# 36 weight pieces of the second block split during the last feed-forward stage and kept in HBM, and one column multiplied once

## The chip, the cores and the metric

The kernel runs on one core of a Trainium2 chip. The metric is the device time of one execution in microseconds (us), as the median of several runs. The core has five engines, each with its own queue of instructions: TensorE (PE, matrix products), VectorE (DVE), ScalarE (ACT), GpSimd (POOL) and SyncE (SP, which here only starts DMAs). DMAs are started from SP, ACT or POOL.

## The reference

512 tokens of 1024 channels go through a first block of two layers and then through a second block. All numbers are float32.

```python
def first_block(x, mem, ...):
    for layer in range(DEPTH):                       # 2
        mix = mixer_ab(...) if layer % 2 == 0 else mixer_c(...)
        x = layer_norm(alpha * x + mix, ...)
        x = layer_norm(alpha * x + cross_attend(x, mem, ...), ...)
        x = layer_norm(alpha * x + conv_ffn(x, ffn_w_up[layer], ...), ...)
    return x

def conv_ffn(x, w_up, conv_w, conv_b, w_down):       # D_FF = 2816 = 22 x 128
    up = x @ w_up
    a, g = up[..., :D_FF], up[..., D_FF:]
    g = causal_dwconv(g, conv_w) + conv_b
    return (jax.nn.gelu(g) * a) @ w_down

def second_block(x, c, ...):                         # one layer
    shift, scale, gate = jnp.split(silu(c) @ w_ada[l] + b_ada[l], 3, axis=-1)
    h = rms_norm(x, norm_g[l]) * (1.0 + scale) + shift
    proj = h @ w_in[l]                               # r, k, v, g, decays; q, k, v, g of the attention
    ps = token_shift(proj[..., :D_SHIFT], mu_shift[l])
    y_r, g_r = rwkv7_mix(ps, ...)                    # a recurrence over the tokens, 8 heads of 64
    y_a = chunk_band_attention(q, ka, va, ...)       # 8 heads of 64
    y = concat([y_r * silu(g_r), y_a * silu(g_a)])
    return x + gate * (y @ w_out[l])
```

## The kernel before

**Products.** PE keeps the accuracy of float32 by splitting each operand into a rounded part `hi` and a rest `lo` and adding three products (`mm3`, lines 263 to 265: `hi*hi`, `hi*lo`, `lo*hi`). A weight matrix comes in *pieces* of 128 x 1024 numbers, 512 KB: one piece is one column block of 128 outputs over all 1024 inputs (for the values of the attention, 256 inputs by 512 outputs), and a piece makes 8 x 3 = 24 products of 128 x 512.

**From a piece to a weight.** `piece` (line 238) takes a buffer `raw` and a slot of the ring of weights (`wtile`), starts the load into `raw` on SP, and calls `split`: ACT copies `hi` into the slot (line 229), and the rest is subtracted by DVE in the first block and by POOL in the second (line 230). In the first block `raw` has three buffers (`raw` 2, `rawx` 1) and the ring six slots (`w` 4, `wx` 2); in the second, two and four.

**The order.** The Tile framework's planner puts the instructions of each engine into a fixed order before the run. It follows the order in which the program emits them as a priority, but takes what is ready by its own estimate of durations; a tile with a tag and `bufs=n` has n buffers, and an instruction waits until one is free. Waits at run time hold up everything behind them on the same engine.

**The last feed-forward** (`ffn(1, ...)`, 1050 to about 1400 us) goes in three chunks of 8, 8 and 6 hidden tiles of 128 channels (`CHUNKS`). An *up stretch* makes two column blocks for each hidden tile f (gate, then value), with ACT and DVE doing the convolution and the gelu behind them (lines 631 to 639) and a split of the result into a tile `hd`. A *down stretch* makes 8 column blocks over the chunk's hidden tiles and adds them to `x` on DVE (lines 645 to 652). The two big tiles `vt` (1 MiB each) hold attention values earlier on and lie idle during this stage.

**The start of the second block.** In `open2`, during the last norm, the column blocks 16, 0, 4, 8 and 1 (`OPEN`) are multiplied by halves of the tokens.

**The second block** (`block2`) has one line of work with long waits, which is emitted at a raised priority: for each of four pairs of heads `rwkv_pair` (a chain through ACT, DVE, POOL and PE, with PE's bonus product at `pb` waiting for DVE's line 894), then `rwkv_invert` (62 steps on DVE, lines 1003 and 1005, between two round trips through HBM), then `rwkv_chain`. All other work is *filler*: `ORDER` lists it by the milestone from which it may be emitted, `bg` holds it as generators, and `fill(us)` emits about that much of it at a place where the line waits. In `ORDER`, r, q, g are column blocks of w_in (each through `lin_g`), v the values (`att_v`, each weight piece read for two halves), p and a the attention, o the start of the output product (`out_begin`, four columns over their first six inputs, whose weights stay in all four slots of `w`), which `out_end` finishes before it makes columns 4 to 7. The entry r1 makes column block 1 again, though `open2` has made it.

Column blocks that `rwkv_epi` shifts go into the ring `rk` of six tiles.

Of the kernel before, what the change touches and what calls it, by code (L numbers as in the profile page):

```python
# [48 lines left out]
    (0, "r1"), (0, "r5"), (0, "r9"),  # L49
# [123 lines left out]
class Prog:  # L173
# [69 lines left out]

    def raw(self):
        self.n += 1
        if self.extra and self.n0 % 3 == 2:
            self.n0 += 1
            return self.t("rawx", [P, 1024], F32, 1)
        self.n0 += 1
        return self.keep.tile([P, 1024], F32, tag="raw", name=f"raw_{self.n}", bufs=2)  # L250

    def wtile(self):
        """The weights' ring: some of its room is there only in the first block."""
        self.nw += 1
        if self.extra and self.nw % (4 + self.extra) >= 4:
            return self.t("wx", [P, 2, 1024], F32R, self.extra)
        self.n += 1
        return self.keep.tile([P, 2, 1024], F32R, tag="w", name=f"w_{self.n}", bufs=4)
# [8 lines left out]
    def lin(self, src, ms, xs, epi, n=S, first=0, last=0):  # L267
        """The first (last) few blocks go through one half of the tokens, then through the other, for the LN
        before (after) them; epi(m, psum, tokens) gets the last ones by halves."""
# [43 lines left out]
    def flush(self):  # L313
        """The LN that is due."""
        while self.pending:
            ts = self.pending.pop(0)
            self.ln_half(ts)
            if self.norm[0] == "ln_ffn_g" and self.norm[2] == 1:
                self.modulate(ts)

    def lin_tm(self, src, pieces, xs, ntok, epi):
        """out[tok tiles][128, 512 cols]: activations stationary, weights moving."""
        banks = [self.bank() for _ in range(ntok)]
        for j, pc in enumerate(pieces):
            w = self.piece(self.a[src][pc])
            for kk in range(2):
                k = 2 * j + kk
                cs = slice(kk * 512, kk * 512 + 512)
                for s in range(ntok):
                    ss = slice(s * P, s * P + P)  # L330
                    self.mm3(banks[s], (xs[k][0][:, ss], xs[k][1][:, ss]), (w[:, 0, cs], w[:, 1, cs]),
                             k == 0, k == 7)
        for s in range(ntok):
            epi(s, banks[s])
# [8 lines left out]
    def rsqrt(self, y, t, v, eps):  # L343
        """y = (v + eps) ** -0.5: the table's value and a Newton step; eps is a column of self.eps."""
# [7 lines left out]
    # residual, then LN over the channels  # L352
# [61 lines left out]
    # mixer of layer 0  # L414
# [204 lines left out]
    def ffn(self, l, xs):  # L619
        nc = self.nc  # L620
        for c, (f0, f1) in enumerate(CHUNKS):
# [3 lines left out]
            def epi(m, ps, ts):  # L625
# [9 lines left out]
                else:  # L635
                    h = self.tmp()
                    nc.vector.tensor_tensor(out=h, in0=ps, in1=keep["g"], op=ALU.mult)
                    hs.append(self.split(self.hd(), h))

# [5 lines left out]
            def epi_d(m, ps, ts):  # L645
# [5 lines left out]
                if c == 1 and l == 0 and m == 1:  # L651
                    self.ada_end()
                if c == 2:
                    self.res_stat(m, ts)
# [5 lines left out]
    # the modulation of the second block, gathered a piece at a time  # L660
# [23 lines left out]
    def ada_end(self):  # L684
        nc = self.nc
        # the sum over the partitions: within 32 of them by turning 32-blocks, then over the four groups
# [18 lines left out]
    def modulate(self, ts):  # L705
        """rms_norm(x) * norm_g * (1 + scale) + shift of half of the tokens."""
# [16 lines left out]
    def open2(self):  # L723
        """The second block's first products, of the first half of the tokens."""
# [48 lines left out]
    # The second block has one line of work with long waits (the states) and much other work for the tensor  # L773
    # engine: `bg` holds the latter as generators, and fill() puts some of it wherever the former waits.
# [57 lines left out]
    def mm(self, out, **kw):  # L832
        """A product on the line with the waits: it stays behind what fill() put before it."""
        self.tc.keep_in_program_order(self.nc.tensor.matmul(out, **kw))  # L834
# [4 lines left out]
    def lin_g(self, src, m, xs, epi, ks=range(KT)):  # L839
        w = self.piece(self.a[src][m])  # L840
# [25 lines left out]
    def rwkv_pair(self, j):  # L866
        """What the chunks of heads 2j and 2j+1 need."""
# [9 lines left out]
        # kk  # L877
# [12 lines left out]
        # k'  # L890
        nc.scalar.activation(u, av, AF.Identity, bias=self.ka1[:, j : j + 1], scale=self.v("k_a_2", j))
        nc.vector.tensor_tensor(out=k, in0=k, in1=u, op=ALU.mult)
        # bonus
# [7 lines left out]
        # decays  # L901
# [20 lines left out]
        # values by token  # L922
# [20 lines left out]
        # scores within the chunks  # L943
# [25 lines left out]
        # keys by token  # L969
# [10 lines left out]
        # the part of the right sides that no state enters  # L980
# [10 lines left out]
    def rwkv_invert(self, prs):  # L991
        """(I - N)^-1 of each chunk's strictly triangular N: 32-blocks by substitution, then the block between."""
# [58 lines left out]
    def rwkv_chain(self, prs, tt):  # L1051
# [40 lines left out]
        def line(i, pr):  # L1092
            for _ in chunks(i, pr):
                yield FILL[9]
            # group norm, then the gate
# [33 lines left out]
    def att_v(self, half, xs):  # L1129
        """Values of two token tiles."""  # L1130
        self.va += [self.t("va", [P, S], F32, 4) for _ in range(2)]
        banks = [self.bank() for _ in range(2)]
        for jj in range(4):
            w = self.piece(self.a["in_va"][jj])
# [12 lines left out]
    def att_epi(self, m, ps):  # L1147
        """Queries or keys of a pair of heads, normed."""
# [15 lines left out]
    def att_probs(self, j):  # L1164
        """Softmax of a pair of heads: a tile holds a chunk's queries of one head, then of the other."""
# [60 lines left out]
    def gate_epi(self, n):  # L1226
        """silu(x) = (tanh(x / 2) + 1) * x / 2; the half comes where it is used."""
# [22 lines left out]
    def out_begin(self):  # L1250
        """The residual, and the first products of w_out over what is there."""
# [5 lines left out]
        for m in range(NPART):  # L1257
            w, ps = self.piece(self.a["out"][m]), self.bank(("mm", "mm", "ch", "ch")[m])
# [9 lines left out]
    def out_end(self, out):  # L1268
        nc = self.nc
        rest = [k for k in range(KT) if k not in KS]  # L1270
        for m in range(8):
# [4 lines left out]
            else:  # L1276
                w, ps = self.piece(self.a["out"][m]), self.bank()
# [93 lines left out]
```

## Time and profile before

| | us |
|---|---|
| median of 3 runs | 1856.47 (1854.88 to 1857.15) |
| span of the profiled execution, first to last instruction | 1854.5 |
| PE busy | 1786.7 |
| DVE busy | 1096.3 |
| ACT busy | 783.0 |
| POOL busy | 362.8 |

The median of the runs is 2.0 us above the span of the profiled execution. A profile's page gives shares over the whole span; the views behind it can be asked for a stretch. In them a group of instructions is named by engine, line, operation, out<-in by the program's names (buffer numbers left out), then shapes and count; then the busy time and the mean of one; then the idle time of the engine ahead of them and what ended it. PE's matrix products are pipelined, so that their shown durations overlap: the distance from start to start tells what one costs. PEld is the loading of weights into PE. The granted clock of PE is shown as a share of 2.4 GHz: 0.50 is 1.2 GHz. A wait for several things is put down to the one that came last.

### The profile page before, as it was taken

To read this page: it belongs to the slowest core of one execution; us is meant where nothing else is said; L and a number is where in the kernel's file an instruction comes from. 1 tells how busy PE (TensorE), PEld (TensorE's weight loads), DVE (VectorE), ACT (ScalarE), POOL (GpSimd) and SP (SyncE) were. 2 spreads that over 40 slices of the span, in tenths; PEclk is the share of its full clock that TensorE was granted. 3 is DMA by queue.
4 is the path that set the end of the run, shared out by engine and by line. 5 is a ranking of instruction groups with operands and counts; after the bars stand their busy time and mean duration, and the time that the engine had idled before them with its cause. 6 is when DMAs were issued, how large, how long until landed. Compare 5 with 4: busy or idle time off the path is not lost.

```text
span 1854.5 us, 26344 instructions
## 1 busy us (share of the span) xinstructions
PE 1786.7 (96%) x10476; PEld 1502.4 (81%) x10476; DVE 1096.3 (59%) x1741; ACT 783.0 (42%) x1319; POOL 362.8 (20%) x331
## 2 busy tenths in 40 slices
PE   8999998999999999999999999999998888879999
PEld 7889988888888888988998988888887766656657
DVE  5676689743463467444565764343447666975673
ACT  5444534532332356232453642232335645535561
POOL 0115014000000051000501400000015455623232
PEclk9999999999999999999999999999999999989999
DMA  8431455332322226333131242323222222222142
GB/s 279 145 103 60 132 181 188 100 102 91 102 92 91 80 64 196 112 96 100 59 104 35 69 125 92 102 92 100 88 86 73 82 75 88 89 74 81 56 160 103
DMA packets 62635, 192.25 MB, mean 104 GB/s; under 512 B 7344, under 2 KB 10032, under 8 KB 62512
## 3 DMA queue, kind: packets, MB, share of 16 engines
q1 hardware_dynamic: 54432, 172.25, 29.0%
q0 software_dynamic: 3248, 9.44, 1.5%
q10 hardware_dynamic: 4832, 8.88, 1.4%
q8 instruction: 82, 1.34, 0.3%
q14 instruction: 41, 0.34, 0.1%
HBM read 181.36 MB, written 9.18 MB: 103 GB/s over the span
## 4 chain that ended last, share of the span: by engine, by line
PE 76%; DVE 15%; ACT 3%; issue 3%; DMA 2%; POOL 0%; SPq 0%; DVEq 0%; ACTq 0%; POOLq 0%
PE ch L264 10%; PE ch L263 10%; PE ch L265 10%; PE mm L263 9%; PE mm L265 9%; PE mm L264 9%; PE pv L264 3%; PE pv L263 3%; PE pv L265 3%; PE ch L834 3%; DVE x L401 2%; DVE xh L405 1%; DVE w L230 1%; DVE x L400 1%; DVE vt L681 1%
## 5 line engine op out<-in xcount | busy, mean ns | idle before, releaser
L263 PE MATMUL mm<-xh,w 128*128 128x512 f32 (+1 forms) x704 | 266.1, 378 | 8.5 <-ACT w L229 7.5
L265 PE MATMUL mm<-xh,w 128*128 128x512 f32 (+1 forms) x704 | 258.6, 367 | 0.8 <-DVE w L230 0.8
L264 PE MATMUL mm<-xh,w 128*128 128x512 f32 (+1 forms) x704 | 259.0, 368 | 0.0
L370 POOL TENSOR_TENSOR t<-x,x 128x512 f32<-128x512 f32 x6 | 8.1, 1351 | 1011.1 <-ACT w L229 656.1
L229 ACT CAST w<-raw 128x1024 fp32r<-128x1024 f32 (+2 forms) x131 | 133.1, 1017 | 164.0 <-PE ch L265 62.9
L263 PEld LDWEIGHTS mm<-xh,w 128*128 128x128 f32 x704 | 135.6, 193 | 35.7 <-ACT w L229 7.8
L264 PE MATMUL ch<-xh,w 128*128 128x512 f32 (+1 forms) x432 | 154.1, 357 | 0.6 <-DVE xh L405 0.5
L264 PEld LDWEIGHTS mm<-xh,w 128*128 128x128 f32 x704 | 135.9, 193 | 22.9 <-issue 3.4
L263 PE MATMUL ch<-xh,w 128*128 128x512 f32 (+1 forms) x432 | 153.0, 354 | 1.3 <-ACT xh L404 1.3
L265 PE MATMUL ch<-xh,w 128*128 128x512 f32 (+1 forms) x432 | 152.7, 353 | 1.5 <-DVE w L230 1.5
L265 PEld LDWEIGHTS mm<-xh,w 128*128 128x128 f32 x704 | 135.8, 193 | 22.6 <-issue 1.1
L229 ACT CAST wx<-raw 128x1024 fp32r<-128x1024 f32 (+1 forms) x85 | 88.1, 1039 | 152.4 <-PE ch L265 71.5
L230 DVE TENSOR_TENSOR w<-rawx,w 128x1024 fp32r<-128x1024 f32 (+2 forms) x85 | 104.1, 1225 | 68.0 <-ACT w L229 67.6
L229 ACT CAST w<-rawx 128x1024 fp32r<-128x1024 f32 (+2 forms) x85 | 87.3, 1027 | 116.4 <-PE mm L265 71.0
L230 DVE TENSOR_TENSOR w<-raw,w 128x1024 fp32r<-128x1024 f32 (+2 forms) x90 | 113.0, 1257 | 37.8 <-ACT w L229 37.4
L230 DVE TENSOR_TENSOR wx<-raw,wx 128x1024 fp32r<-128x1024 f32 (+1 forms) x85 | 107.6, 1267 | 27.6 <-ACT wx L229 27.4
L230 POOL TENSOR_TENSOR w<-raw,w 128x1024 fp32r<-128x1024 f32 x41 | 100.4, 2456 | 119.0 <-ACT w L229 115.1
L263 PE MATMUL ch<-xh,wx 128*128 128x512 f32 (+1 forms) x304 | 103.5, 341 | 0.0
L265 PE MATMUL ch<-xh,wx 128*128 128x512 f32 (+1 forms) x304 | 103.0, 339 | 0.0
L264 PE MATMUL ch<-xh,wx 128*128 128x512 f32 (+1 forms) x304 | 103.0, 339 | 0.0
L263 PE MATMUL mm<-hd,w 128*128 128x256 f32 (+1 forms) x304 | 97.7, 322 | 3.6 <-ACT hd L229 3.6
L265 PE MATMUL mm<-hd,w 128*128 128x256 f32 (+1 forms) x304 | 97.9, 322 | 0.0
(484 smaller groups left out, 4498.6 us busy)
## 6 DMA issues: line engine op xcount, KB each, us to landing
raw<-in_up SPq DMA_DIRECT2D x56, 512.0 KB, 3.5
rawx<-in_up SPq DMA_DIRECT2D x32, 512.0 KB, 3.5
kt<-in_ada SPq DMA_DIRECT2D x48, 256.0 KB, 3.3
raw<-in_dn SPq DMA_DIRECT2D x24, 512.0 KB, 3.5
raw<-in_in_r SPq DMA_DIRECT2D x24, 512.0 KB, 3.5
raw<-in_c_in SPq DMA_DIRECT2D x16, 512.0 KB, 3.5
raw<-in_xo SPq DMA_DIRECT2D x12, 512.0 KB, 3.6
raw<-in_xv SPq DMA_DIRECT2D x11, 512.0 KB, 4.1
```

What stands on the lines that cost most here:

```text
L229: nc.scalar.copy(hi, src)
L230: (eng or nc.vector).tensor_tensor(out=lo, in0=src, in1=f32(hi), op=ALU.subtract)
L263: mm(out, lhsT=ah, rhs=bh, start=start, stop=False)
L264: mm(out, lhsT=ah, rhs=bl, start=False, stop=False)
L265: mm(out, lhsT=al, rhs=bh, start=False, stop=stop)
L370: eng.tensor_tensor(out=sz, in0=self.x[0][:, ts] if m == 1 else sz, in1=z, op=ALU.add)
L400: (nc.vector if k in DVE_SUB else nc.gpsimd).tensor_tensor(out=x, in0=x, in1=mn, op=ALU.subtract)
L401: nc.vector.scalar_tensor_tensor(out=x, in0=x, scalar=gk, in1=rs, op0=ALU.mult, op1=ALU.mult)
L405: nc.vector.scalar_tensor_tensor(out=lo, in0=x, scalar=bk, in1=f32(hi), op0=ALU.add, op1=ALU.subtract)
L681: nc.vector.scalar_tensor_tensor(out=dst, in0=raw, scalar=sc, in1=dst, op0=ALU.mult, op1=ALU.add)
L834: self.tc.keep_in_program_order(self.nc.tensor.matmul(out, **kw))
```

## The change

The column block r1 is taken out of `ORDER`. During the last feed-forward, 36 of the second block's weight pieces are loaded, split and written back to HBM as pairs (`hi`, `lo`), one after another: `pre_begin` lists them in the order of their use, and `pre_step` is called once for each hidden tile of an up stretch and once for each column block of the first two down stretches, 38 times in all. A step starts the load of the next piece into the second half of a tile `vt` from POOL's queue and, for the piece of the step before, lets ACT copy `hi` into the first half, POOL subtract `lo` in place, and POOL's queue store both halves (1 MiB). In the second block `ready` loads a pair straight into a slot of `w` from SP's queue, in place of `piece`: 40 loads of 1 MiB, since the 4 pieces of the values are read twice. The remaining lines of the diff only shorten comments.

```diff
 ORDER = (
-    (0, "r1"), (0, "r5"), (0, "r9"),
+    (0, "r5"), (0, "r9"),
...
+    def pre_begin(self):
+        self.prep, todo = {}, []
+        for _, ws in ORDER:
+            for w in ws.split("+"):
+                k, m = w[0], int(w[1:])
+                if k in "rq" and m not in OPEN:
+                    todo.append(("in_r", m))
+                elif k == "g":
+                    todo.append(("in_r", 12 + m) if m < 4 else ("in_ga", m - 4))
+                elif w == "v0":
+                    todo += [("in_va", i) for i in range(4)]
+                elif k == "o":
+                    todo += [("out", i) for i in range(8)]
+        self.todo, self.due2 = todo, []
+
+    def pre_step(self):
+        nc = self.nc
+        if self.todo:
+            key = self.todo.pop(0)
+            t = self.t("vt", [P, 2, D], F32, 2)
+            nc.gpsimd.dma_start(out=t[:, 1, :], in_=self.a[key[0]][key[1]])
+            self.due2.append((key, t))
+        if len(self.due2) > 1 or not self.todo:
+            for key, t in self.due2[:1]:
+                self.due2.pop(0)
+                hi, lo = t[:, 0, :].bitcast(F32R), t[:, 1, :].bitcast(F32R)
+                nc.scalar.copy(hi, t[:, 1, :])
+                nc.gpsimd.tensor_tensor(out=lo, in0=t[:, 1, :], in1=t[:, 0, :], op=ALU.subtract)
+                name = f"sp_{key[0]}{key[1]}"
+                d = self.prep[key] = self.dram.tile([P, 2, D], F32, tag=name, name=name)
+                nc.gpsimd.dma_start(out=d, in_=t)
+
+    def ready(self, src, m):
+
+        w = self.wtile()
+        self.nc.sync.dma_start(out=f32(w), in_=self.prep[src, m])
+        return w
+
...
     def ffn(self, l, xs):
         nc = self.nc
+        if l == 1:
+            self.pre_begin()
...
                     hs.append(self.split(self.hd(), h))
+                    if l == 1:
+                        self.pre_step()
...
+                if c < 2 and l == 1:
+                    self.pre_step()
                 if c == 2:
                     self.res_stat(m, ts)
...
     def lin_g(self, src, m, xs, epi, ks=range(KT)):
-        w = self.piece(self.a[src][m])
+        w = self.ready(src, m)
...
-            w = self.piece(self.a["in_va"][jj])
+            w = self.ready("in_va", jj)
...
-            w, ps = self.piece(self.a["out"][m]), self.bank(("mm", "mm", "ch", "ch")[m])
+            w, ps = self.ready("out", m), self.bank(("mm", "mm", "ch", "ch")[m])
...
-                w, ps = self.piece(self.a["out"][m]), self.bank()
+                w, ps = self.ready("out", m), self.bank()
```

## Rows read from the trace of the kernel before

**Rows 1.** The page, part 1: busy us, share, count of each engine.

```profile
PE 1786.7 (96%) x10476; PEld 1502.4 (81%) x10476; DVE 1096.3 (59%) x1741; ACT 783.0 (42%) x1319; POOL 362.8 (20%) x331
```

**Rows 2.** Stretches: from:to, length, each engine's busy us, clock, DMA share, GB/s.

```profile
1094.00:1380.00 286.00, 286.00 (x1251) 234.64 (x1250) 121.89 (x141) 86.51 (x107) 0.00 (x0) 1.00 0.29 94
1440.00:1661.00 221.00, 190.51 (x1035) 144.47 (x1033) 164.95 (x262) 108.93 (x158) 112.67 (x79) 0.92 0.26 82
...
1780.00:1854.00 74.00, 67.58 (x305) 51.44 (x303) 39.29 (x53) 27.07 (x34) 20.37 (x11) 1.00 0.32 111
```

**Rows 3.** PE's waits from 1440 to 1700 us: total, times, longest.

```profile
PE ch L834 <- DVE rt L894: 17.8, 4, 4.9
PE at L1157 <- ACT t L1153: 6.0, 2, 5.8
```

**Rows 4.** The stretches at half clock from 1435 us on, as in rows 2.

```profile
1435.60:1442.40 6.80, 6.10 (x16) 5.03 (x17) 3.22 (x7) 4.27 (x11) 0.00 (x0) 0.50 0.40 135
...
1633.50:1640.30 6.80, 3.34 (x6) 2.01 (x7) 6.59 (x12) 3.22 (x5) 2.36 (x1) 0.50 0.00 0
1654.00:1660.80 6.80, 5.30 (x14) 3.98 (x14) 4.04 (x7) 0.63 (x1) 3.52 (x9) 0.50 0.44 125
sum 40.80, PE 33.53 PEld 22.94 DVE 32.56 ACT 10.81 POOL 21.35; mean PE 4.79 PEld 3.28 DVE 4.65 ACT 1.54 POOL 3.05
```

**Rows 5.** POOL's groups from 1100 us on, shapes apart.

```profile
L230 POOL TENSOR_TENSOR w<-raw,w 128x1024 fp32r<-128x1024 f32 x41 | 100.4, 2456 | 119.0 <-ACT w L229 115.1 <-DMA raw<-in_in_r 3.5
...
L966 POOL DMA_DIRECT2D dn<-mk x16 | 9.3, 588 | 12.2 <-DVE mk L960 12.2
```

**Rows 6.** DVE in time, about the inversion: start us, us, line, operation.

```profile
1604.40 4.37 DVE L349 TENSOR_SCALAR t<-t 128x512 f32<-128x512 f32 x1
...
1610.95 2.33 DVE L1003 TENSOR_TENSOR rt<-c,c 128x87 f32<-128x87 f32 x1
...
1615.67 0.28 DVE L1003 TENSOR_TENSOR rt<-c,c 128x112 f32<-128x112 f32 x1
...
1633.15 0.42 DVE L349 TENSOR_SCALAR t<-t 128x512 f32<-128x512 f32 x1
```

**Rows 7.** POOL in time, in the inversion.

```profile
1610.74 4.79 POOL L230 TENSOR_TENSOR w<-raw,w 128x1024 fp32r<-128x1024 f32 x2 [2.28 <-ACT w L229]
```

**Rows 8.** DVE in time, in pair 0.

```profile
1471.97 2.07 DVE L921 COPY pc<-rt 128x8 f32<-128x8 f32 x1
...
1476.23 2.96 DVE L894 SCALAR_TENSOR_TENSOR rt<-rk,vec,rk 128x512 f32<-128x512 f32 x1
```

**Rows 9.** POOL in time, in pair 0.

```profile
1471.15 2.85 POOL L230 TENSOR_TENSOR w<-raw,w 128x1024 fp32r<-128x1024 f32 x1
```

**Rows 10.** ACT in time, in pair 0.

```profile
1468.95 1.04 ACT L229 CAST w<-raw 128x1024 fp32r<-128x1024 f32 x1
```

**Rows 11.** PE in time, as output column 4 starts.

```profile
1828.86 0.39 PE L263 MATMUL mm<-ar,w 128*128 128x512 f32 x1
...
1831.58 0.39 PE L263 MATMUL mm<-xh,w 128*128 128x512 f32 x1
```

**Rows 12.** Filler ahead of pair 0's bonus product: PE, PEld, DVE, ACT on tiles mm.

```profile
1461.60:1479.30 17.70, 12.69 (x52) 9.69 (x52) 1.13 (x3) 1.38 (x2) 1.00 0.34 114
```

**Rows 13.** DVE's groups from 1440 us on, shapes apart.

```profile
L1113 DVE SCALAR_TENSOR_TENSOR yy<-yy,sav 128x512 f32<-128x512 f32 x4 | 4.8, 1195 | 0.1
```

**Rows 14.** DVE in time, where the first up stretch turns to down.

```profile
1135.86 0.68 DVE L230 TENSOR_TENSOR hd<-t,hd 128x512 fp32r<-128x512 f32 x1
```

**Rows 15.** PE in time at that turn: the last hidden tile's first product.

```profile
1138.33 0.39 PE L263 MATMUL pv<-hd,wx 128*128 128x512 f32 x1
```

**Rows 16.** ACT in time: the first slot's cast after the partial columns.

```profile
1825.03 1.06 ACT L229 CAST w<-raw 128x1024 fp32r<-128x1024 f32 x1 [6.65 <-PE mm L265]
```

**Rows 17.** DMA issues: out<-in, queue, count, KB each, median us to landing.

```profile
raw<-in_out SPq DMA_DIRECT2D x8, 512.0 KB, 3.6
...
dt<-c POOLq DMA_DIRECT2D x1, 512.0 KB, 2.9
```

## Prediction: what the change does to the time

> **What bounds the kernel now.** I read the page's busy shares first: TensorE (PE) is busy for 1786.7 us of a span of 1854.5 [rows 1], so a change pays only where it takes products away, closes an idle gap of PE or ends a stretch at the lower clock. The table of stretches says where those are [rows 2]. In the last feed-forward (1094 to 1380 us) PE is busy for 286.00 of 286 us, ScalarE (ACT) for 86.51, VectorE (DVE) for 121.89, GpSimd (POOL) for 0.00. In the second block up to the end of the inversion (1440 to 1661 us) PE is busy for 190.51 of 221 us at a granted clock of 0.92: 30.5 us are idle. The list of waits names the gaps [rows 3]: 17.8 us in four waits for the bonus input of a pair (DVE L894), 6.0 for the norm of a query or key (L1157). Behind such gaps the clock is down at 1.2 GHz: seven stretches of 40.8 us, the first in the norm before the block, with 33.53 us of busy PE [rows 4]. The six inside the block hold 33.53 - 6.10 = 27.4 us, which cost half of that, 13.7.
>
> **What stretches those chains.** Each of the 41 pieces of the block costs POOL a subtract of 2.456 us, 100.4 us in all [rows 5], and ACT a cast of 1.04. In the inversion a DVE step of 0.28 us or less takes 2.33 when a subtract runs beside it [rows 6, 7]: the step at 1610.95 us ends where the first of two subtracts ends. There are five such steps, each some 2.1 us too long, 10.6 in all, and just before them one norm step of L349 takes 4.37 us where it needs 0.42 at 1633.15: 3.9 more. In pair 0 the copy L921, of 8 columns, takes 2.07 us and ends with the subtract that runs from 1471.15 to 1474.00 us; L892, next on DVE, is late with it, and ACT's cast at 1468.95 us stands ahead of the exponential that L921 needs [rows 8 to 10].
>
> **The change part by part.**
> *r1 gone.* 24 products fall away; twelve take 1831.58 - 1828.86 = 2.72 us [rows 11], so **5.4 us**. No wait loses its cover, since filler isn't bound to its place: before pair 0's bonus product 52 filler products ran [rows 12], while the budgets of the two fills ahead of it (1.12 and 3, at 0.65 a step) make 2 + 5 steps, 21 products. The planner brought work forward, and can bring r2.
>
> *Pair waits.* Without subtract and cast L921 needs no more than 0.28 us and L892 starts some 1.9 earlier. What stays is POOL's own work of a pair, behind which L894 takes 2.96 us [rows 8]. So 4 x 1.9 = **7.6 us** of 17.8. Bounds: nothing, if POOL's pair products, freed, collide earlier; all 17.8, if L894 too finds POOL free.
>
> *Clock in the pairs.* The four low stretches behind them hold 33.53 - 6.10 - 3.34 - 5.30 = 18.8 us of busy PE [rows 4], 9.4 lost. The gaps that I leave are about 2.5 us each. Whether the clock falls behind those no row tells: the tail has 6.4 idle us at a clock of 1.00 [rows 2], in smaller gaps. I take half, **4.7 us**, with 0 and 9.4 as ends.
>
> *Inversion.* 14.5 us come off DVE, more than the 6.0 us for which PE waits for norms queued behind these steps. I take **5.9 us**, and 1.7 for half of the 3.34 at the low clock behind it: **7.6**.
>
> *Tail.* L1113 takes 1195 ns on average [rows 13] where a split of the same size with two inputs takes 0.68 us [rows 14]: 4 x 0.5, **2.0 us**.
>
> *Added to the feed-forward.* 36 x 1.04 = 37 us of ACT, 36 x 2.456 = 88 us of POOL, and 72 POOL DMAs at 0.59 us of issue [rows 5], 42 us. The cover is 200 idle us of ACT and an idle POOL. The DMA engines move 94 GB/s at a share of 0.29 [rows 2], 324 when full; 36 x 1.5 MiB over some 300 us add 189: 283. In a down stretch, with a step per 5.6 us, the demand is 375, which lags some 7 us behind by its end; the next up stretch takes that back. The weights are safe: six slots, five pieces ahead, 28 us. A stall can come where up turns to down: the last hidden tile is split until 1136.54 us and needed at 1138.33 [rows 14, 15], 1.8 us of slack. A cast and a subtract ahead of it (1.04 + 2.42) would stall 1.7. Between 0 and 3 x 1.7 I take **+1.5 us**. The Trainium skill, "SBUF — State Buffer", section "Who interferes with whom", makes the ports that VectorE and GpSimd share an exclusive lock, also against a VectorE instruction with two SBUF inputs. That rule speaks against the change, since the splits of the feed-forward are such instructions and meet no POOL today; the inversion's rows agree with it (2.33 us for 0.28). By it every turn would pay and the term be 5.1.
>
> *Loads of 1 MiB.* They go straight into a slot of `w`, of which there are four. In full work a piece lasts 5.4 us and three lie ahead, 16 us: covered. In `out_end` all four hold partial columns. The first is free when its cast starts, at 1825.03 us, and column 4 starts at 1828.86 [rows 11, 16]: 3.8 us. 512 KB land in 3.6 us [rows 17], so 1 MiB in 3.6 to 7.2; at 324 GB/s the second half adds 1.6. I take 5.2, so **+1.4 us** (0 to 3.4). The Trainium skill, "DMA: Bandwidth & Descriptors", section "Bandwidth", gives 6.15 us for 1 MB (from GpSimd's queue, not SP's): by it the term would be 2.4; no row shows it. The inversion's own DMAs now meet larger ones: **+1 us** (0 to 3).
>
> *Sum.* 5.4 + 7.6 + 4.7 + 7.6 + 2.0 = 27.3 gained, 3.9 lost: 23.4. The span becomes 1831.1; the median of the runs, 1856.47, lies 2.0 above today's span: **1833 us**.
>
> **The rivals.**
> *Gaps close wholly.* Idle 30.5, low clock 13.7, r1 5.4, tail 2.0, less 3.9: 47.7, **1809 us**. For it: a weight subtract stands ahead of the four waits. Against: L894's own delay behind POOL's pair products.
> *Gaps form again.* POOL's pair products start earlier and hold DVE as long, and the clock stays low: r1, half of the inversion and the tail are left, 5.4 + 3.8 + 2.0 - 3.9 = 7.3: **1849 us**. For it: L894 at 2.96 us with no weight subtract beside it. Against: L921, where one was.
> *The preparation stalls the feed-forward.* On POOL's one queue a step loads piece n, then subtracts and stores piece n-1; with two `vt` buffers load n waits for store n-2. If this order stays as written, a step lasts the subtract, two issues and the store: 2.5 + 1.2 + S. 512 KB are stored in 2.9 us [rows 17], so S is 2.9 to 5.8 and a step 6.6 to 9.5 us, against 5.6 in a down stretch and 11.2 in an up stretch. ACT's added casts then wait for POOL, with the casts of the weights queued behind them. After two down stretches with an up between, the lag is 24p - 179: 28 us, the weights' whole lead, at a step of p = 8.6. From there it costs: 21 us at 9.5, 38 at 10.2 with contention, and the clock with it. Price 40: **1873 us**. Against it: the planner brings forward what is ready, and with the subtract ahead of the waiting load two buffers, each round some 12 us, make 6 to 7 us a step.
>
> **How the numbers follow.** Forecast (1833, by itself 1822 to 1843) 0.55; gaps form again 0.20; gaps close 0.12; stall 0.10; the prepared pieces save nothing anywhere 0.03. The range holds the forecast, the re-formed gaps and what lies just short of full closing, 1811 to 1851, and leaves out the stall and the far end. A measurement of this kernel tells 0.2%, 3.7 us, from no change. Faster by more: 0.55 + 0.20 + 0.12 = 0.87; same 0.03; slower 0.10.
>
> **What would show it.** Right: no weight subtract on POOL in the block, inversion steps all under 0.5 us, pair waits of 2 to 3 us, PE full from 1094 to 1380 us with some 88 us of POOL beside it. Wrong: idle PE at an up-to-down turn, or in the second down stretch with ACT waiting for a DMA into `vt`; L894 still 3 us late; products that wait for a DMA into `w` anywhere but ahead of column 4.

## The result, and the profile of the changed kernel

The changed kernel takes 1888.1 us (median of 4 runs, 1880.9 to 1892.2) against 1855.7 for the kernel before: a ratio of 1.017, with an interval of 1.015 to 1.019. It is 32 us slower, where the forecast was 23 us faster. The time lies outside the range on record (1811 to 1851). Nearest to what happened is the rival called "the preparation stalls the feed-forward", which had a chance of 0.10 and a price of 1873 us. ScalarE is held up by the added casts, as it says; but what TensorE then waits for are hidden tiles, from the first down stretch on, where the rival had the weights run out late.

The profiled execution spans 1887.2 us, 32.7 more than before. Its busy shares answer to [rows 1]: TensorE does 24 products fewer, and is busy 2.5 us longer all the same.

```profile
span 1887.2 us, 26394 instructions
PE 1789.2 (95%) x10452; PEld 1501.9 (80%) x10452; DVE 1092.7 (58%) x1739; ACT 777.9 (41%) x1313; POOL 389.0 (21%) x398
```

The next table splits the span at points that both traces have: the first product of the cross-attention's output, the three down stretches (products on the tiles `hd`), and the first product of the second block's chain (the helper `mm`, L834 before, L879 after). All numbers are differences of starts and ends in the traces.

| stretch, us | before | after | difference |
|---|---|---|---|
| cross-attention's output to first down stretch | 142.1 | 157.6 | +15.5 |
| first down stretch | 45.0 | 71.7 | +26.7 |
| second up stretch | 86.9 | 98.5 | +11.6 |
| second down stretch | 44.9 | 52.2 | +7.3 |
| from there to the chain's first product | 150.4 | 146.4 | -4.0 |
| second block | 393.9 | 368.0 | -25.9 |

The block gained 25.9 us, and the stages ahead of it lost 57.1. The table of stretches says the same of TensorE (columns as in [rows 2]: from:to, length, each engine's busy us, granted clock, DMA share, GB/s). First the stretch that was full before, then the first down stretch alone, and below it the same down stretch in the kernel before:

```profile
1094.00:1380.00 286.00, 251.79 (x1059) 202.02 (x1059) 130.72 (x121) 99.28 (x117) 90.99 (x77) 0.92 0.64 228
1150.40:1222.10 71.70, 48.82 (x194) 37.76 (x193) 26.27 (x23) 20.76 (x23) 27.93 (x24) 0.81 0.66 244
```

```profile
1133.40:1178.40 45.00, 45.00 (x194) 36.20 (x194) 15.92 (x17) 8.93 (x9) 0.00 (x0) 1.00 0.31 102
```

From 1094 to 1380 us TensorE is busy for 251.79 us of 286, where it had been busy for 286.00. In the down stretch the same products (192, and one over each edge) keep it busy for 48.82 us, at a granted clock of 0.81, and 22.9 us are idle. What it waits for, from 985 to 1480 us (total, times, longest), is one thing above all: the high half of a hidden tile, which ScalarE splits at L229.

```profile
PE pv L302 <- ACT hd L229: 25.8, 4, 16.2
PE at L427 <- POOL t L409: 5.2, 2, 3.4
PE mm L302 <- ACT w L229: 3.0, 1, 3.0
```

The second row belongs to the norm ahead of the feed-forward, whose sums GpSimd makes (L409); the third is the only wait for a weight's cast.

And ScalarE, in the same stretch, waits for the loads of the pieces that are prepared (L271 is the new cast), 120 us in the three rows together:

```profile
ACT vt L271 <- DMA vt<-in_in_r: 61.2, 13, 9.8
ACT vt L271 <- DMA vt<-in_out: 33.8, 5, 9.4
...
ACT vt L271 <- DMA vt<-in_in_ga: 25.1, 3, 12.9
```

Line by line, at the start of that down stretch (start us, us, engine, line, operation; in brackets the idle time before it and what ended it), ScalarE:

```profile
1143.68 0.63 ACT L229 CAST hd<-t 128x512 fp32r<-128x512 f32 x1
1150.91 1.06 ACT L271 CAST vt<-vt 128x1024 fp32r<-128x1024 f32 x1 [6.61 <-DMA vt<-in_in_r]
1154.98 1.05 ACT L271 CAST vt<-vt 128x1024 fp32r<-128x1024 f32 x1 [3.01 <-DMA vt<-in_in_r]
...
1160.18 0.62 ACT L229 CAST hd<-t 128x512 fp32r<-128x512 f32 x1 [0.24 <-DVE t L678]
1170.24 1.05 ACT L271 CAST vt<-vt 128x1024 fp32r<-128x1024 f32 x1 [9.45 <-DMA vt<-in_in_r]
...
1178.69 0.62 ACT L229 CAST hd<-t 128x512 fp32r<-128x512 f32 x1 [1.76 <-DVE t L678]
```

TensorE, which takes up that last split at once:

```profile
1179.37 0.80 PE L302 MATMUL pv<-hd,wx 128*128 128x512 f32 x1 [16.22 <-ACT hd L229]
```

and GpSimd, whose queue issues loads (L265) and stores (L275):

```profile
1140.22 0.58 POOL L275 DMA_DIRECT2D sp_in_r<-vt  x1 [0.30 <-POOL vt L272]
1142.33 0.54 POOL L265 DMA_DIRECT2D vt<-in_in_r  x1 [1.54 <-DMA sp_in_r<-vt]
1146.36 0.54 POOL L265 DMA_DIRECT2D vt<-in_in_r  x1 [3.49 <-DMA sp_in_r<-vt]
```

A load waits until the store before last has left the buffer; its cast starts 8.6 us after its issue (1142.33 to 1150.91, 1146.36 to 1154.98 us); and the splits of the hidden tiles stand behind the casts. From 1150.91 to 1170.24 us a round of two pieces takes 19.3 us here. The DMA rows have the load at 6.1 and 6.9 us, where the row that the forecast had, from SP's queue and without a store beside it, shows 3.6 [rows 17]:

```profile
vt<-in_in_r POOLq DMA_DIRECT2D x20, 512.0 KB, 6.1
...
vt<-in_out POOLq DMA_DIRECT2D x8, 512.0 KB, 6.9
```

How far ScalarE's queue had run ahead is seen by counting casts. The program puts one step behind each hidden tile's split, with a lag of one; so six or seven casts belong before the eighth split, which comes at 1178.7 us. The group of L271 up to that time holds 20, and begins in the cross-attention's output:

```profile
L271 ACT CAST vt<-vt x20: 1034/1050/1060, 1000.5 to 1172.0; 128x1024 fp32r<-128x1024 f32 x20
```

The theory is then: **the planner fixed an order for ScalarE in which casts stand far ahead of their place in the program, at a pace that the loads don't keep; each late load holds up the split of a hidden tile, and TensorE behind it.** Rivals: the copies and subtracts as such (VectorE and GpSimd slowing each other, ScalarE's time); the DMA traffic, 228 GB/s where it was 94; the product r1, which is gone, as a cover for something.

### The profile page after: what moved, and what is told of

Read it like the earlier page. It is cut to its first block, busy times and chain, and to the rows that moved or that the text cites. A ratio compares the mean times of both kernels' runs of the same rounds, so it can differ in the third digit from the quotient of the medians.

```text
span 1887.2 us, 26394 instructions
## 1 busy us (share of the span) xinstructions
PE 1789.2 (95%) x10452; PEld 1501.9 (80%) x10452; DVE 1092.7 (58%) x1739; ACT 777.9 (41%) x1313; POOL 389.0 (21%) x398
## 4 chain that ended last, share of the span: by engine, by line
PE 61%; DVE 14%; DMA 13%; issue 5%; ACT 4%; POOL 3%; ACTq 0%; SPq 0%; DVEq 0%; POOLq 0%
PE ch L302 8%; PE ch L303 8%; PE ch L304 8%; PE mm L302 7%; PE mm L303 7%; PE mm L304 7%; DMA vt<-in_in_r 3%; PE pv L303 3%; PE pv L302 3%; PE pv L304 3%; PE ch L879 3%; POOL vt L272 2%; DMA sp_in_r<-vt 2%; DMA vt<-in_out 2%; DVE x L440 2%
## 5 line engine op out<-in xcount | busy, mean ns | idle before, releaser
L302 PE MATMUL mm<-xh,w 128*128 128x512 f32 (+1 forms) x696 | 262.9, 378 | 11.7 <-ACT w L229 11.5
L304 PE MATMUL mm<-xh,w 128*128 128x512 f32 (+1 forms) x696 | 255.6, 367 | 1.8 <-DVE w L230 1.8
L303 PE MATMUL mm<-xh,w 128*128 128x512 f32 (+1 forms) x696 | 256.1, 368 | 0.0
L230 DVE TENSOR_TENSOR w<-rawx,w 128x1024 fp32r<-128x1024 f32 (+2 forms) x85 | 111.9, 1317 | 96.6 <-ACT w L229 96.2
L302 PEld LDWEIGHTS mm<-xh,w 128*128 128x128 f32 x696 | 134.4, 193 | 38.7 <-ACT w L229 12.1
L409 POOL TENSOR_TENSOR t<-x,x 128x512 f32<-128x512 f32 x6 | 8.7, 1449 | 741.7 <-ACT w L229 459.0
L303 PEld LDWEIGHTS mm<-xh,w 128*128 128x128 f32 x696 | 134.7, 194 | 22.9 <-issue 3.5
L304 PEld LDWEIGHTS mm<-xh,w 128*128 128x128 f32 x696 | 134.0, 193 | 23.6 <-DVE w L230 2.8
L230 DVE TENSOR_TENSOR w<-raw,w 128x1024 fp32r<-128x1024 f32 (+2 forms) x90 | 121.2, 1347 | 46.9 <-ACT w L229 46.4
L230 DVE TENSOR_TENSOR wx<-raw,wx 128x1024 fp32r<-128x1024 f32 (+1 forms) x85 | 116.6, 1373 | 40.0 <-ACT wx L229 39.7
L229 ACT CAST wx<-raw 128x1024 fp32r<-128x1024 f32 (+1 forms) x85 | 88.0, 1039 | 121.8 <-PE ch L304 54.4
L229 ACT CAST w<-raw 128x1024 fp32r<-128x1024 f32 (+2 forms) x90 | 90.3, 1005 | 107.5 <-PE ch L304 45.2
L229 ACT CAST w<-rawx 128x1024 fp32r<-128x1024 f32 (+2 forms) x85 | 87.4, 1028 | 93.0 <-PE mm L304 54.2
L272 POOL TENSOR_TENSOR vt<-vt 128x1024 fp32r<-128x1024 f32 x36 | 87.7, 2435 | 75.0 <-ACT vt L271 74.7
```

The costliest lines, as they stand in the source:

```text
L229: nc.scalar.copy(hi, src)
L230: (eng or nc.vector).tensor_tensor(out=lo, in0=src, in1=f32(hi), op=ALU.subtract)
L272: nc.gpsimd.tensor_tensor(out=lo, in0=t[:, 1, :], in1=t[:, 0, :], op=ALU.subtract)
L302: mm(out, lhsT=ah, rhs=bh, start=start, stop=False)
L303: mm(out, lhsT=ah, rhs=bl, start=False, stop=False)
L304: mm(out, lhsT=al, rhs=bh, start=False, stop=stop)
```

## The experiments

**One part alone: r1.** The kernel before with the first column's product taken out of the list, and no preparation.

```diff
-    (0, "r1"), (0, "r5"), (0, "r9"),
+    (0, "r5"), (0, "r9"),
```

> The kernel before without r1 and nothing else. Theory: 24 products of 0.227 us fall away and filler is brought forward in their place, so 1855.7 - 5.4 = 1850 us (1846 to 1854). Rival: r1 covered a wait of pair 0, and the gap grows by what is taken out: 1855 to 1860 us.

Measured: 1847.8 us against 1854.5, ratio 0.997 (0.995 to 0.998). The block is 388.5 us long, 5.4 less than before, which is what 24 products at the rows' pace were to save. The loss isn't r1's.

**The copy on GpSimd.** Loads, stores and subtracts stay; only ScalarE no longer waits.

```diff
-                nc.scalar.copy(hi, t[:, 1, :])
+                nc.gpsimd.tensor_copy(hi, t[:, 1, :])
```

> The changed kernel with the copy of the rounded half moved from ACT to POOL, so that no engine but POOL waits for a load into vt; the DMAs and subtracts stay. Theory (ACT's queue is held by casts that wait for these loads): the 48 us lost within the feed-forward go, the 10 us lost in the norm before it stay or grow a little, 1835 to 1850 us. Rival 1 (the DMA traffic delays the weights) and rival 2 (POOL's subtracts hold VectorE): nothing changes, 1880 to 1895 us.

Measured: 1849.7 us, ratio 0.997 (0.995 to 0.998), 38 us less than the changed kernel. The feed-forward is all but full again, at clock 1.00, with more GpSimd work in it (129.54 us) and no fewer bytes a second:

```profile
1094.00:1380.00 286.00, 285.37 (x1261) 234.37 (x1260) 149.71 (x145) 89.18 (x109) 129.54 (x106) 1.00 0.71 245
```

So within the feed-forward neither the traffic nor GpSimd's work costs TensorE more than 0.6 us. VectorE does pay: it is busy 27.8 us longer than before [rows 2]. Ahead of the first down stretch 10.9 us of idle TensorE are left; the longest of them is a wait of 5.0 us for a sum of the norm on GpSimd (L409).

**The traffic alone.** No copy and no subtract; each piece is loaded and stored twice over as it came, so the second block multiplies by weights whose halves aren't split.

```diff
-                nc.scalar.copy(hi, t[:, 1, :])
-                nc.gpsimd.tensor_tensor(out=lo, in0=t[:, 1, :], in1=t[:, 0, :], op=ALU.subtract)
...
-                nc.gpsimd.dma_start(out=d, in_=t)
+                nc.gpsimd.dma_start(out=d, in_=t[:, 1, :].unsqueeze(1).to_broadcast([P, 2, D]))
```

> The changed kernel without the copy and the subtract: pieces are loaded into vt and stored as they came, twice over, so the weights of the second block are not split and the output is not the reference's. Theory (ACT waits): PE is full in the feed-forward, total 1825 to 1845 us. Rival 1 (DMA traffic): the feed-forward stays 40 to 60 us longer than before, 1870 us or more.

Measured: 1829.7 us (one run), the block at 367.5 and the feed-forward full (row below).

**The work alone.** Copies and subtracts in the program's place on tiles that stay in SBUF, no load and no store; the block splits its pieces itself as before.

```diff
-            t = self.t("vt", [P, 2, D], F32, 2)
-            nc.gpsimd.dma_start(out=t[:, 1, :], in_=self.a[key[0]][key[1]])
+            t = self.vts[len(self.todo) % 2]
...
-                nc.scalar.copy(hi, t[:, 1, :])
+                self.tc.keep_in_program_order(nc.scalar.copy(hi, t[:, 1, :]))
...
```

> The feed-forward makes the 36 copies on ACT and 36 subtracts on POOL on two tiles that stay in place, each at its place in the program, without the loads and stores; the second block loads and splits its own pieces as before, so nothing prepared is used. Theory (ACT waits for DMAs): without a DMA to wait for there is no stall, 1848 to 1856 us. Rival 2 (subtracts hold VectorE) or plain work on ACT: 1870 us or more.

Measured: 1847.3 us (one run), as r1 alone. The two rows of 1094 to 1380 us, the traffic's kernel first:

```profile
1094.00:1380.00 286.00, 286.00 (x1252) 234.72 (x1251) 122.36 (x141) 86.98 (x107) 24.46 (x40) 1.00 0.60 208
```

```profile
1094.00:1380.00 286.00, 286.00 (x1251) 234.61 (x1250) 126.73 (x142) 118.96 (x141) 86.87 (x33) 1.00 0.30 92
```

TensorE is full in both. The second row has ScalarE's casts and 33 of GpSimd's 36 subtracts in it, 87 us, and VectorE's busy time is 4.8 us above [rows 2]. In this stretch each part alone is free for TensorE; what is left is the two together, a cast that waits for its load. The casts of this run stand in the program's place; casts brought forward with no load to wait for were not run.

**Loads held behind the norm.** The load of each piece stays behind what the program put on GpSimd's queue before it, so no step can begin in the cross-attention's output.

```diff
-            nc.gpsimd.dma_start(out=t[:, 1, :], in_=self.a[key[0]][key[1]])
+            self.tc.keep_in_program_order(nc.gpsimd.dma_start(out=t[:, 1, :], in_=self.a[key[0]][key[1]]))
```

> The changed kernel, with the loads of the vt tiles kept on GpSimd's queue behind what the program put there before them, so that the planner can't bring a preparation step forward into the norm ahead of the feed-forward; the cast stays on ScalarE. Theory (two losses: ScalarE's queue held by a cast whose load is late, and steps brought forward into the norm): only the second one goes, some 6 to 10 us of idle TensorE ahead of the first down stretch; that stretch stays near 72 us long; 1872 to 1884 us in all. Rival (the steps brought forward are the cause of the whole loss): the down stretches return to 45 us and the time is near 1833.

Measured: 1894.6 us, ratio 1.021 (1.019 to 1.023). The part on the norm held: the first down stretch starts 142.3 us after the cross-attention's output, as before the change, with 0.6 us idle on the way. The time expected was wrong. The casts start 64 us later, at 1065.0 us, so all 36 fall into the feed-forward and the last cast comes at 1359.6 us instead of 1311.5; the second down stretch too is now 75.2 us long. Twelve casts come before the eighth split, fewer than 20, and the loss is larger: it doesn't follow the count. ScalarE now holds TensorE up for longer than the norm had cost:

```profile
PE pv L302 <- ACT hd L229: 46.5, 4, 16.2
```

**Loads held, and the copy on GpSimd.** Both edits together.

> The changed kernel with the high half copied by GpSimd in place of ScalarE, and the loads of the vt tiles pinned as in the run before. Theory: both losses go; TensorE idles some 7 to 10 us between the cross-attention's output and the second block, as in the kernel before, the block keeps its gain of 25 us: 1828 to 1838 us, faster than both kernels. Rival (the work of the preparation as such costs the feed-forward): no better than the copy on GpSimd alone, near 1850.

Measured: 1834.2 us, ratio 0.988 (0.987 to 0.990), faster than both kernels. The stage from the cross-attention's output to the block is 476.9 us long (469.3 before, 526.4 in the changed kernel); the block is 367.1 (368.0 in the changed kernel).

**The copy on VectorE.** Another engine that works in order and on which hidden tiles depend.

```diff
-                nc.scalar.copy(hi, t[:, 1, :])
+                nc.vector.tensor_copy(hi, t[:, 1, :])
```

> The changed kernel with the high half copied by VectorE in place of ScalarE. Theory (any engine that works off its instructions in order and on which the next hidden tile depends is held up by a cast that waits for its load): VectorE stalls as ScalarE did, the first down stretch is 60 to 75 us long, 1870 to 1895 us. Rival (ScalarE's own copy, its time or its place among the activations, is the cause): the down stretches are 45 us and the time is near 1850, as with the copy on GpSimd.

Measured: 1888.1 us, ratio 1.017 (1.014 to 1.020). The first down stretch is 69.4 us long, and the waits for the loads have moved with the copy. TensorE's longest waits are still for ScalarE's split of a hidden tile (16.3 us in two), which now comes late because VectorE's part of the convolution, ahead of it, does (ScalarE waits 81.9 us for that, at L672):

```profile
DVE vt L271 <- DMA vt<-in_in_r: 35.6, 9, 9.1
DVE vt L271 <- DMA vt<-in_out: 29.7, 5, 7.8
DVE vt L271 <- DMA vt<-in_in_ga: 17.3, 3, 8.7
```

ScalarE is not the point; being the engine behind whose wait a hidden tile stands is.

**Steps in the up stretches alone.** 21 pieces are prepared, the other 15 treated as before the change.

```diff
+        if (src, m) not in self.prep:
+            return self.piece(self.a[src][m])
...
-                if c < 2 and l == 1:
-                    self.pre_step()
```

> The changed kernel with preparation steps in the up stretches alone, where a step comes about every 11 us: 21 pieces are prepared, the other 15 are loaded and split in the second block as before the change; the cast stays on ScalarE. Theory (a step takes 8.6 us by its loads and stores and stalls only where steps come faster than that): the down stretches are 45 us again, the loss ahead of the feed-forward (10 us) stays; the block gains two thirds of its 20 us: 1842 to 1854 us. Rival (each cast on ScalarE stalls by itself): 21 of 36 of the loss stay, and the time is 1865 to 1880.

Measured: 1860.4 us, ratio 1.003 (1.002 to 1.004), 6 us above what the theory gave. My picture was still that a step runs about where the program has it, every 11 us. It doesn't: before the eighth split there are as many casts as in the changed kernel,

```profile
L271 ACT CAST vt<-vt x20: 1029/1047/1056, 997.2 to 1165.4; 128x1024 fp32r<-128x1024 f32 x20
```

and the first down stretch is 70.9 us long again. With the last of the 21, at 1181.3 us, the trouble ends: the other two down stretches take 45.0 and 44.2 us. Steps fewer and farther apart in the program don't keep the first down stretch free as long as the planner may bring them together.

**All of a step held in place.** Load (as above), cast (on ScalarE) and subtract stay behind what the program put there before them; all 36 pieces.

```diff
...
-                nc.scalar.copy(hi, t[:, 1, :])
-                nc.gpsimd.tensor_tensor(out=lo, in0=t[:, 1, :], in1=t[:, 0, :], op=ALU.subtract)
+                self.tc.keep_in_program_order(nc.scalar.copy(hi, t[:, 1, :]))
+                self.tc.keep_in_program_order(nc.gpsimd.tensor_tensor(out=lo, in0=t[:, 1, :], in1=t[:, 0, :], op=ALU.subtract))
```

> The changed kernel with the load, the cast (on ScalarE still) and the subtract of each preparation step kept behind what the program put there before them on their engines, so that a step stands where the program has it and not ahead. Theory (the loss is ScalarE held by casts that the planner placed ahead of their place: 20 of them before the eighth hidden tile's split, where the program has 7): the up stretches, a step every 11 us against 8 us that a piece takes, run without idle time; in the down stretches eight steps ask for 64 us where there are 45, so 5 to 15 us may be lost at each of the two turns to the next up stretch; 1838 to 1862 us. Rival (a cast on ScalarE stalls wherever it stands): 1880 to 1895 us.

Measured: 1835.0 us, ratio 0.988 (0.986 to 0.991): 53 us less than the changed kernel by the order of three instructions, and 3 us below the range expected. Only six casts come before the eighth split. ScalarE's waits for the loads are no shorter than in the changed kernel, 124 us in three rows (1040 to 1400 us):

```profile
ACT vt L271 <- DMA vt<-in_in_r: 61.6, 15, 6.9
ACT vt L271 <- DMA vt<-in_out: 36.4, 8, 6.5
ACT vt L271 <- DMA vt<-in_in_ga: 26.3, 4, 9.1
```

but TensorE's wait for a hidden tile is down from 25.8 us to one of 6.7, at the turn to the third down stretch:

```profile
PE ch L302 <- ACT hd L229: 6.7, 1, 6.7
```

Neither turn to the next up stretch loses anything, where 5 to 15 us were expected. The profiled execution is the longest of the four (1842.0 us), so this wait may be shorter in the others. What a wait on ScalarE costs is thus set by what stands behind it, and not by its length. No run holds the cast alone in place; with the loads alone held the loss stayed.

**The same with steps in the up stretches alone.** All three instructions held in place, 21 pieces.

> Preparation steps in the up stretches alone (21 pieces prepared, 15 loaded and split in the second block as before the change), all three instructions of a step kept in the program's place, the cast on ScalarE. Theory: a step every 11 us against 8 us for a piece leaves no stall anywhere; TensorE idles under 12 us from the cross-attention's output to the second block, and the block is no longer than with the steps not pinned (361 us): 1826 to 1838 us. Rival (a cast on ScalarE stalls wherever it stands): 1850 to 1862 us, as without the pins.

Measured: 1818.5 us, ratio 0.980 (0.978 to 0.982), the fastest of all, 36 us below the kernel before and 7.5 below the range expected. No wait for a hidden tile's cast is left in the feed-forward, and TensorE is full there:

```profile
1094.00:1380.00 286.00, 286.00 (x1251) 234.54 (x1250) 124.65 (x142) 104.24 (x126) 68.92 (x57) 1.00 0.56 194
```

Its block is 360.4 us long, 7.6 less than with 36 prepared pieces. Most of that is one wait in the inversion, shown in the next section.

**All of a step held in place, on GpSimd.**

> All 36 pieces, the copy on GpSimd, and the load, the copy and the subtract kept in the program's place on GpSimd's queue. Theory: the 6 us that TensorE idled ahead of the first down stretch with only the loads pinned came from subtracts and copies beside the norm's last steps; with the first step later they go: 1824 to 1834 us. Rival: those 6 us have another cause and stay, 1832 to 1838 us.

Measured: 1845.1 us, ratio 0.995 (0.993 to 0.997), worse than with the loads alone held and outside both ranges. The idle time ahead of the first down stretch went from 6.1 to 2.8 us, the way the theory had it, but the same fault appeared on the new engine: at 9.9 us a piece the steps reach into the third down stretch, where GpSimd has the sums of the next norm (L409) to do, and those stand behind the last pieces.

```profile
1401.15 0.53 POOL L265 DMA_DIRECT2D vt<-in_out  x1 [3.88 <-DMA sp_out<-vt]
...
1409.78 0.58 POOL L275 DMA_DIRECT2D sp_out<-vt  x1 [0.30 <-POOL vt L272]
1410.38 1.27 POOL L409 TENSOR_TENSOR t<-x,x 128x512 f32<-128x512 f32 x1
```

```profile
PE at L427 <- POOL t L409: 19.2, 2, 19.0
```

The profiled execution is the longest of ten (1855.8 us, 1839.6 to 1855.8), so 19.0 us is rather the most that this wait takes than its usual length.

## Why the prediction was wrong, point by point

**The step that failed: "Added to the feed-forward", +1.5 us; the stages ahead of the block lost 57.1.** Three things in it were wrong.

*"The cover is 200 idle us of ACT."* Idle time covers work only where the work is ready when its turn comes. The casts weren't: they wait for a DMA, and whatever ScalarE has behind them waits too. The prediction counted a cast ahead of the last hidden tile as 1.04 us; with its wait it was up to 12.9 longer. ScalarE's wait for a DMA into `vt` it named only among the signs of being wrong, and priced it nowhere outside the rival. The Trainium skill states the rule that decides this, in "PSUM — Partial Sum Buffer", section "Engine vs sequencer instructions": the queues of ScalarE, VectorE and GpSimd are strictly first in, first out. The traces agree: in the changed kernel the split at 1160.18 us follows the two late casts, and with the copy on VectorE or, late in the stage, on GpSimd, the stall came from those engines (16.3 us for hidden tiles, 19.0 for the norm).

*"Against it: the planner brings forward what is ready."* It does bring forward, but by a model, when the order is fixed, and not by what is ready on the chip. I had put this on the side of the forecast; it is the cause of the loss. Left to the planner, 20 casts come before the eighth split, and the time is 1888.1 us; held in place, six, and 1835.0. It also brought the first steps into the norm ahead of the feed-forward, where GpSimd and VectorE both have work of their own; holding the loads back took away the whole 15.5 us there. I had kept the preparation between 1094 and 1380 us without a row that said it would stay there.

*The round of a piece.* I had a round of some 12 us for two pieces, 6 to 7 us a step. Measured from the first cast to the last, 1000.5 to 1311.5 us, 35 intervals: 8.9 us a piece, 17.8 for two. A load takes 6.1 to 6.9 us there, and the row that I had says 3.6 [rows 17]: that is about half of the 5.8 us by which my round was too short. The store was within its bounds: the rival took 2.9 to 5.8 us, and the stores of 1 MiB landed in 4.6 to 5.3 (medians).

**The nearest rival, and its threshold.** "From there it costs" was put at 8.6 us a step with the steps in the program's order. The kernel with all of a step held in place is that case: (1377.4 - 1075.3) / 35 = 8.6 us, near the rival's sum of 2.5 + 1.2 and a store of 5.1 us, and it loses 6.7 us to a wait, late, at the third turn; its stages ahead of the block are 11.3 us longer than before. That part was about right. The changed kernel lost 46 us more, and early, at nearly the same step: for 8.9 us a piece the rival's sum gives 24 x 8.9 - 179 - 28 = 6.6 us. The threshold says nothing of casts that stand out of their place. So the price of 40 us stood on a delay of the weights that this kernel doesn't show, and was too low; the chance of 0.10 rested on the wrong reason.

**The clock.** In the first down stretch the granted clock is at 1.2 GHz (0.50) from 1156.9 to 1184.3 us, where TensorE is busy for 6.66 of 27.4 us; most of its first gap (6.1 us, to 1160.85) and all of its second (16.2 us, to 1179.37) lie in it. The products of that stretch take 48.82 us where they took 45.00 at the full clock. So 3.8 of the 26.7 us are the clock's, the rest is idle.

**The second block: right in the main, 24.9 forecast with its two small losses, 25.9 measured.** The parts below make 5.4 + 7.7 + 6.0 + 5.2 + 2.0 - 2.0 = 24.3 us; the other 1.6 are not assigned. Part of the agreement is luck: the clock gave more than forecast, the inversion and column 4 less. The waits of TensorE from 1455 us on, to be read against [rows 3]:

```profile
PE ch L879 <- DVE rt L939: 10.1, 4, 2.9
PE ch L879 <- DVE rt L1072: 6.4, 1, 6.4
...
PE mm L302 <- DMA w<-sp_out: 2.0, 1, 2.0
```

- *r1*, 5.4 us: the kernel without it alone has a block 5.4 us shorter.
- *Pair waits*, 7.6 of 17.8 us: 17.8 to 10.1, 7.7. The bonus input (L894, now L939) still takes 3.0 us beside GpSimd's own work of the pair, as foreseen.
- *Clock in the pairs*, 4.7 us, half of the possible: of the four low stretches two are left, of 3.4 us each, so some 6 of 9.4 came back.
- *Inversion*, 7.6 us with 1 lost to its DMAs: 5.2. The norm waits (6.0 us) are gone and the steps run at 0.19 to 0.43 us. The clock gave 2.3: behind the inversion 8.64 us of busy PE were at the half clock [rows 4], now 4.09. But TensorE's wait for the round trip behind the inversion grew from 3.3 us to 6.4. Before:

```profile
PE ch L834 <- DVE rt L1027: 3.3, 1, 3.3
```

  The cause was named and mis-sized: its DMA now meets loads of 1 MiB. `dt<-c` landed in 2.9 us before [rows 17]; after, from 1560 to 1720 us:

```profile
c<-dn POOLq DMA_DIRECT2D x1, 512.0 KB, 6.2
dt<-c POOLq DMA_DIRECT2D x1, 512.0 KB, 6.5
```

  With steps in the up stretches alone the pieces near that point are loaded as 512 KB again. There `c<-dn` still lands in 6.4 us but `dt<-c` in 2.9, the wait is 0.5 us and the block 7.6 us shorter. All thirteen traces agree: `dt<-c` takes 6.5 to 6.8 us in the eight that load 1 MiB there, 2.9 in the other five.

```profile
c<-dn POOLq DMA_DIRECT2D x1, 512.0 KB, 6.4
dt<-c POOLq DMA_DIRECT2D x1, 512.0 KB, 2.9
```

- *Tail*, 2.0 us: L1113 (now L1158) took 1195 ns [rows 13] and takes 690, four times 0.5.

```profile
L1158 DVE SCALAR_TENSOR_TENSOR yy<-yy,sav 128x512 f32<-128x512 f32 x4 | 2.8, 690 | 0.1
```

- *Column 4*, 1.4 us: 2.0. The loads concerned landed in 5.7 us, where I had 5.2:

```profile
w<-sp_out SPq DMA_DIRECT2D x8, 1024.0 KB, 5.7
```

  The Trainium skill's 6.15 us for 1 MB ("DMA: Bandwidth & Descriptors", section "Bandwidth") gave 2.4, so the measured 2.0 lies between; the other loads of 1 MiB landed in 4.8 to 4.9 us.

**The page that spoke against the change.** The exclusive lock of "SBUF — State Buffer", section "Who interferes with whom" in the Trainium skill, was to cost 5.1 us at the turns. With all copies and subtracts in the program's place and without the preparation's DMAs, TensorE was full from 1094 to 1380 us. In the feed-forward no run here shows that price on TensorE. On VectorE it shows: the split of a hidden tile (L230) takes 685 ns on average from 1094 to 1380 us before, and 1125 with the copy on GpSimd, 0.44 us more, less than the 1.8 us of slack that the prediction read at the turn. In the norm ahead it reaches TensorE: of four steps in a row on VectorE (L440) of the changed kernel, the two beside a subtract of GpSimd take 2.49 and 3.70 us, at 1039.62 and 1042.91 us, the last alone 0.47; and with the copy on GpSimd and the loads held TensorE waits 4.8 us for the norm's steps on VectorE (L444). These rows agree with the rule; what it costs TensorE comes in the norm and not at the turns.

## What to carry to other kernels

Idle time of an engine hides added work only if that work is ready when its turn comes; an instruction that waits for a DMA in a queue that works in order holds up all that stands behind it, so count what stands behind it before the wait's length. Where a planner fixes the order, ask where it will put the new steps, not where the program has them, and hold a slow transfer's consumer in place or give it to an engine on which nothing near depends. Take a transfer's time from a row with the same queue and the same neighbours.

## What was not expected of the hardware

- A load of 512 KB on GpSimd's queue landed in 4.7 to 7.3 us (medians of four groups) among stores of 1 MiB and the weights in the changed kernel, and in 3.9 to 4.8 in the kernel with all steps held in place, which moves more bytes in the same stretch (269 GB/s against 228). The cause is open; no run issues these loads from another queue.
- A transfer of 512 KB of the inversion beside loads of 1 MiB took 6.2 and 6.5 us, without them 3.6 and 2.9: 1.7 and 2.2 times as long, at 313 and 218 GB/s.
- 87 us of GpSimd subtracts beside 127 us of VectorE work in the feed-forward lengthened VectorE's busy time by 4.8 us only; with the copy on GpSimd too and the loads and stores there, it was 27.8 us, and in the second block single steps of 0.28 us had taken 2.33 [rows 6].
